# Differential attention in a two-block kernel: the softmax sum kept on VectorE, outputs copied unscaled in pairs, the norm taken once per head, and key copies moved to GpSimd

## The chip, the cores and the metric

The kernel runs on one core of a Trainium2 chip. The metric is the device time of one execution in microseconds. The engines are named as in the profile: PE is TensorE, PEld its weight loads, DVE is VectorE, ACT is ScalarE, POOL is GpSimd, SP is SyncE.

## The reference, cut to what matters

The program is a stack of transformer blocks on 512 tokens of width 1024, with 256 context tokens beside them. The change lies in one layer of the second part, whose mixer runs two attentions side by side: a neighbourhood attention with 8 heads of 64 columns, and a differential attention with 4 heads. A differential head has two queries and two keys of 64 columns and one value of 128 columns:

```python
def diff_attend(q1, q2, k1, k2, v, lam):
    scale = q1.shape[-1] ** -0.5
    p1 = jax.nn.softmax(jnp.einsum('bhqd,bhsd->bhqs', q1, k1).astype(F32) * scale, axis=-1)
    p2 = jax.nn.softmax(jnp.einsum('bhqd,bhsd->bhqs', q2, k2).astype(F32) * scale, axis=-1)
    return jnp.einsum('bhqs,bhsd->bhqd', (p1 - lam * p2).astype(v.dtype), v)
...
y_l = jnp.concatenate([merge_heads(ya_l), merge_heads(rms_norm(yb_l, subln) * (1.0 - lam_init))],
                      axis=-1) @ w_out
```

Tokens attend to 768 keys (512 tokens and 256 context), context tokens to the 256 context keys alone. Each output row of 128 columns is divided by its root mean square and multiplied by a gain row.

## The kernel before, in words

The layer's attentions are one software pipeline. `diff_attention` makes 24 items, 4 heads (`hd`) by 6 query tiles (`t`) of 128 rows: tiles 0 to 3 are **long** (768 keys, six blocks of 128), tiles 4 and 5 are **short** (256 keys, two blocks). `neighbourhood` adds its items behind them. `skewed` runs the list so that at step i the stage s of item i-s is issued, the deepest stage first; within that, the tile framework's scheduler decides the order in which each engine's queue takes the instructions. An engine takes its queue strictly in order.

The stages of a differential item, with the lines of the profile:

- `load`: at tile 0 of a head `stacked` prepares the head's keys (two f32r copies `whi`, `wlo`, whose other halves hold remainders, subtracted by GpSimd at L1585, and two high parts `kz`, copied by ScalarE at L1589, one per half of the partitions). For each tile `doubled` prepares the query: ScalarE copies, GpSimd subtracts `ql` (L1597) and twice `qd` (L1599). `stacked` with `kz` also serves the neighbourhood pairs and the dilated attention of the first block.
- `score`: for each of the two halves PE computes the scores (L1610) into one of two PSUM buffers, VectorE takes the row maximum (L900), ScalarE the exponential with its row sum (L901) into a tile `E`, VectorE the reciprocal of that sum (L904). Then VectorE makes the factor `er` (L1785) and adds the second exponential, times that factor, to the first: columns 0 to 511 on VectorE (L1787), columns 512 to 767 on GpSimd (a product L1791 and an addition L1792). Short items have the VectorE part only, of 256 columns.
- `turn`: PE transposes the sum (L436), ScalarE (L1628) and VectorE (L1630) copy the result from PSUM to the tile `PT`, of which there are three.
- `apply`: PE multiplies by the values into a `pv` bank (L1802), ScalarE copies the 128 columns to `da_o`, scaled by the reciprocal row sum (L1805), and squares them with a row sum (L1806).
- `norm`, once per head: VectorE works out the reciprocal root of 6 columns (L298 to L304, L1810) and multiplies the head's 128x768 tile `da_o` twice, by that root (L1812) and by the gain row (L1813).
- `end`, four steps later: PE transposes `da_o` (L436), and ScalarE and VectorE split it into the operand of the output projection (L319, L320).

After the last head the neighbourhood items follow in the same queues, so the last head's norm and end lie among them.

## Time and profile before

| what | us |
| --- | --- |
| runs | 2574.99, 2583.11, 2584.61 (median 2583.11) |
| profiled execution | 2572.39 |
| span of the profiled execution | 2570.6 |
| the differential items, in that span | about 1088 to 1206 |
| the last head's transposes of `da_o` | 1210.65 |

The profile is of one execution; all times in it are microseconds from the start of its span, or ns where marked. The rows of the page and of the trace on which the text rests stand in the section on rows. A busy column gives the time in which an engine was executing, with the number of instructions in brackets. PEclk is the granted share of full clock on TensorE. In a row of the order in time, the bracket at the end is how long the engine stood idle ahead of it, and whose result ended that.

### The profile page before, as it was taken

Reading aid. Unit: us, or ns where it says so; the run is one execution under the profiler, and the core shown is the slowest. Engines: PE = TensorE matmul, PEld = TensorE weight load, DVE = VectorE, ACT = ScalarE, POOL = GpSimd, SP = SyncE. Lnnn points to the kernel's source line nnn. Section 1 sums busy time; section 2 is a strip of 40 time slices with the busy share of each in tenths; the row PEclk is TensorE's granted clock in tenths of the full one; section 3 lists DMA queues with packets and bytes.
Section 4 is the critical chain, followed back from the end, with each engine's and each line's share of the span. In section 5 each row is a group of like instructions: output and inputs, shape, how many; then the busy total and the mean of one; then the engine's idle time right before and its main releaser. Section 6 shows DMA issues by size and latency. Waiting matters only on the chain.

```text
span 2570.6 us, 35341 instructions
## 1 busy us (share of the span) xinstructions
PE 2454.1 (95%) x13312; PEld 2036.7 (79%) x13312; DVE 1629.0 (63%) x2896; ACT 995.9 (39%) x1763; POOL 1197.7 (47%) x835
## 2 busy tenths in 40 slices
PE   8899999999999999877999999999999999999999
PEld 6668776878887777766888888888888888788887
DVE  6944648677775686588755876777576465534333
ACT  4435435322224423377633222122244563323222
POOL 3356536455556455587633332323245326344443
PEclk9999999999999899998999999999999999999999
DMA  5230023344444332301232333424242113232332
GB/s 192 74 111 14 29 72 131 117 166 138 152 162 138 132 107 85 103 17 32 72 120 82 121 138 107 140 92 155 74 132 82 34 60 138 82 95 84 106 101 91
DMA packets 105773, 262.13 MB, mean 102 GB/s; under 512 B 12017, under 2 KB 20337, under 8 KB 105220
## 3 DMA queue, kind: packets, MB, share of 16 engines
q1 hardware_dynamic: 105028, 258.84, 30.1%
q8 instruction: 105, 1.72, 0.3%
q10 hardware_dynamic: 576, 1.05, 0.1%
q14 instruction: 64, 0.52, 0.1%
HBM read 248.15 MB, written 16.93 MB: 103 GB/s over the span
## 4 chain that ended last, share of the span: by engine, by line
PE 75%; DVE 13%; POOL 3%; issue 3%; ACT 3%; DMA 2%; SPq 1%; POOLq 0%; ACTq 0%; DVEq 0%
PE ps_mm L326 15%; PE ps_mm L324 15%; PE ps_mm L325 15%; PE ps_mx L324 3%; PE ps_mx L325 3%; PE ps_mx L326 3%; PE ps_m L324 3%; PE ps_m L326 3%; PE ps_m L325 3%; PE ps_pv L1617 2%; PE ps_t L436 2%; PE ps_s L1610 2%; DVE cv_y L538 1%; POOL wlo L313 1%; PE ps_p L757 1%
## 5 line engine op out<-in xcount | busy, mean ns | idle before, releaser
L313 POOL TENSOR_TENSOR wlo<-wraw,whi 128x1024 fp32r<-128x1024 f32 (+2 forms) x344 | 783.5, 2281 | 1064.9 <-ACT whi L312 981.0
L312 ACT ACTIVATE whi<-wraw 128x1024 fp32r<-128x1024 f32 (+2 forms) x345 | 336.8, 978 | 892.0 <-PE ps_mm L325 470.1
L324 PE MATMUL ps_mm<-h,whi 128*128 128x512 f32 (+1 forms) x1496 | 539.9, 362 | 10.8 <-ACT whi L312 7.4
L326 PE MATMUL ps_mm<-h,wlo 128*128 128x512 f32 (+1 forms) x1496 | 538.6, 361 | 1.9 <-POOL wlo L313 1.9
L325 PE MATMUL ps_mm<-h,whi 128*128 128x512 f32 (+1 forms) x1496 | 538.9, 361 | 1.1 <-DVE h L1163 1.0
L324 PEld LDWEIGHTS ps_mm<-h,whi 128*128 128x128 f32 x1496 | 281.9, 189 | 56.5 <-ACT whi L312 7.4
L326 PEld LDWEIGHTS ps_mm<-h,wlo 128*128 128x128 f32 x1496 | 281.5, 188 | 49.2 <-POOL wlo L313 2.5
L325 PEld LDWEIGHTS ps_mm<-h,whi 128*128 128x128 f32 x1496 | 281.7, 188 | 46.4 <-DVE h L1163 1.5
L325 PE MATMUL ps_mm<-fa,whi 128*128 128x512 f32 (+1 forms) x528 | 187.5, 356 | 0.0
L326 PE MATMUL ps_mm<-fa,wlo 128*128 128x512 f32 (+1 forms) x528 | 186.2, 356 | 1.2 <-POOL wlo L313 1.2
L324 PE MATMUL ps_mm<-fa,whi 128*128 128x512 f32 (+1 forms) x528 | 185.6, 356 | 0.0
L1288 DVE SCALAR_TENSOR_TENSOR cb<-ps_mm,small,cb 128x511 f32<-128x511 f32 (+1 forms) x66 | 43.6, 660 | 186.8 <-ACT cb L1286 186.8
L1236 DVE SCALAR_TENSOR_TENSOR x<-ps_mm,mod,x 128x512 f32<-128x512 f32 x80 | 59.5, 749 | 136.6 <-PE ps_mm L326 129.7
L1109 DVE CUSTOM_DVE_ANT_0 ada_j<-ada_w,ada_c 128x512 f32<-128x512 f32 x128 | 134.5, 1051 | 7.0 <-DMA ada_w<-in_w_ada 6.7
L1109 DVE CUSTOM_DVE_ANT_0 ada_w<-ada_w,ada_c 128x512 f32<-128x512 f32 x128 | 129.5, 1012 | 3.5
L1109 DVE CUSTOM_DVE_ANT_0 x<-x 128x512 f32<-128x512 f32 x128 | 124.9, 996 | 1.9
L326 PEld LDWEIGHTS ps_mm<-fa,wlo 128*128 128x128 f32 x528 | 98.9, 188 | 17.8 <-POOL wlo L313 1.8
L324 PEld LDWEIGHTS ps_mm<-fa,whi 128*128 128x128 f32 x528 | 98.9, 188 | 16.4 <-ACT whi L312 0.3
L325 PEld LDWEIGHTS ps_mm<-fa,whi 128*128 128x128 f32 x528 | 99.2, 188 | 16.0
L900 DVE TENSOR_REDUCE nm<-ps_s 128x1 f32<-128x768 f32 (+1 forms) x96 | 73.9, 774 | 34.9 <-PE ps_s L1610 33.7
L436 PE MATMUL ps_t<-ident,E 128*128 128x128 f32 x464 | 77.7, 287 | 15.1 <-POOL E L1792 9.2
L325 PE MATMUL ps_mx<-h,whi 128*128 128x512 f32 x216 | 85.5, 396 | 3.8 <-DVE h L993 3.8
(500 smaller groups left out, 5207.5 us busy)
## 6 DMA issues: line engine op xcount, KB each, us to landing
wraw<-in_w_up SPq DMA_DIRECT2D x88, 512.0 KB
ada_w<-in_w_ada SPq DMA_DIRECT2D x128, 256.0 KB
wraw<-in_w_d SPq DMA_DIRECT2D x48, 384.0 KB
wraw<-in_w_d SPq DMA_DIRECT2D x53, 320.0 KB
x<-in_w_ada SPq DMA_DIRECT2D x64, 256.0 KB
wraw<-in_we_in SPq DMA_DIRECT2D x24, 512.0 KB
wraw<-in_w_g SPq DMA_DIRECT2D x22, 512.0 KB
wraw<-in_w_u SPq DMA_DIRECT2D x22, 512.0 KB
```

Source lines behind the costliest of these rows:

```text
L312: self.S.activation(hi[:, :n], raw[:, :n], AF.Copy)
L313: (eng or self.G).tensor_tensor(out=lo[:, :n], in0=raw[:, :n], in1=hi.bitcast(F32)[:, :n], op=ALU.subtract)
L324: mm(ps, lhi, rhi, start=start, stop=False)
L325: mm(ps, lhi, rlo, start=False, stop=False)
L326: mm(ps, llo, rhi, start=False, stop=stop)
L436: last = self.PE.transpose(ps[:, j * P:(j + 1) * P], src[:, j * P:(j + 1) * P], self.ident)
L900: V.tensor_reduce(out=m, in_=src, op=ALU.max, axis=AX.X, negate=True)
L1109: V.tensor_tensor_reduce(out=(junk, w)[s], in0=w, in1=c[:, s, i * T:i * T + T], scale=0.5, scalar=0.0, op0=ALU.mult, op1=ALU.add, accum_ou ...
L1236: V.scalar_tensor_tensor(out=xs[s][:, m], in0=p[:, :w], scalar=mod[:, gate * 8 + m, s:s + 1], in1=xs[s][:, m], op0=ALU.mult, op1=ALU.add)
L1288: V.scalar_tensor_tensor(out=cb[:, t0 + 1:t1], in0=pg[s][:, :w_ - 1], scalar=fw[0], in1=cb[:, t0 + 1:t1], op0=ALU.mult, op1=ALU.add)
L1610: self.PE.matmul(p[:, c0:min(n, c0 + 512)], q[i], k[i][:, c], start=i == 0, stop=i == 1)
L1617: self.PE.matmul(pv[64 * e:64 * e + 64, cols], vals(e, kt), pts[e][:, kt * P:(kt + 1) * P], start=kt == 0, stop=kt == nk - 1)
```

## The change

The sum of the two exponentials is made by one VectorE instruction over all columns, 768 or 256; the two GpSimd instructions are gone. The reciprocal row sums of the first half are kept for a whole head in a tile `da_r`. The `pv` bank is one PSUM bank for the whole stage with four slots of 128 columns, and ScalarE copies two items' outputs at once, unscaled (128x256); it squares nothing. The norm is then taken per head: GpSimd squares the 128x768 tile (L1810 of the kernel after), VectorE sums it by tiles (L1812), multiplies twice by `da_r` (L1814), works out the root and multiplies it by `da_r` (L1817), and GpSimd does the two products over 128x768 (L1818, L1819). `end` comes two steps later than before. In `stacked` the two `kz` copies are made by GpSimd instead of ScalarE; this holds for all callers (24 copies in the program).

```diff
         for e, (own, other) in enumerate(HALVES):
-            self.S.activation(kz[own, e], src[own], AF.Copy)
+            self.G.tensor_copy(kz[own, e], src[own])
...
-                    c = slice(0, min(n, T))
-                    V.scalar_tensor_tensor(out=e1[:, c], in0=e2[:, c], scalar=r2, in1=e1[:, c], op0=ALU.mult,
+                    V.scalar_tensor_tensor(out=e1[:, :n], in0=e2[:, :n], scalar=r2, in1=e1[:, :n], op0=ALU.mult,
                                            op1=ALU.add)
-                    if n > T:
-                        c = slice(T, n)
-                        G.tensor_scalar(out=e2[:, c], in0=e2[:, c], scalar1=r2, scalar2=None, op0=ALU.mult)
-                        G.tensor_tensor(out=e1[:, c], in0=e1[:, c], in1=e2[:, c], op=ALU.add)
...
-                    pv = self.bank(ps, "pv")
+                    if hd == t == 0:
+                        st["v"] = self.bank(ps, "pv")
...
+                    c = (6 * hd + t) % 4 * P
                     for kt in range(nk):
-                        PE.matmul(pv[:, :P], st["t", hd, t][:, kt * P:(kt + 1) * P],
+                        PE.matmul(st["v"][:, c:c + P], st["t", hd, t][:, kt * P:(kt + 1) * P],
                                   vb[:, kt + k0 // P, hd * P:(hd + 1) * P], start=kt == 0, stop=kt == nk - 1)
-                    sq = at.tile([P, P], F32, name="da_q", bufs=1)
-                    S.activation(st["o", hd][:, t], pv[:, :P], AF.Copy, scale=r1)
-                    S.activation(sq, st["o", hd][:, t], AF.Square, accum_out=st["s", hd][:, t:t + 1])
+                    if t % 2:
+                        S.activation(st["o", hd][:, t - 1:t + 1].rearrange("p a b -> p (a b)"), st["v"][:, c - P:c + P],
+                                     AF.Copy)
...
+                    sq = at.tile([P, 6 * P], F32, name="PT", bufs=3)
+                    G.tensor_tensor(out=sq, in0=flat, in1=flat, op=ALU.mult)
+                    ssq = at.tile([P, 6], F32, name="da_s")
+                    V.tensor_reduce(out=ssq, in_=sq.rearrange("p (a b) -> p a b", b=P), op=ALU.add, axis=AX.X)
+                    for _ in range(2):
+                        V.tensor_tensor(out=ssq, in0=ssq, in1=r1, op=ALU.mult)
                     V.tensor_scalar(out=ssq, in0=ssq, scalar1=1.0 / P, scalar2=EPS, op0=ALU.mult, op1=ALU.add)
                     r = self.rsqrt(at, ssq, 6, "da")
-                    V.tensor_tensor(out=o, in0=o, in1=self.lastb(r, P), op=ALU.mult)
-                    V.tensor_tensor(out=o, in0=o, in1=self.midb(sub, 6), op=ALU.mult)
+                    V.tensor_tensor(out=r, in0=r, in1=r1, op=ALU.mult)
+                    G.tensor_tensor(out=o, in0=o, in1=self.lastb(r, P), op=ALU.mult)
+                    G.tensor_tensor(out=o, in0=o, in1=self.midb(sub, 6), op=ALU.mult)
...
                 items.append([load, None, score, None, turn, apply, norm if last else None, None, None, None,
...
-                              end if last else None])
+                              None, None, end if last else None])
```

The order that results is shown at two places. The first is GpSimd's queue where the scores pass from head 1 to head 2. `kz1` and `kz0` are the two sets of high parts, `qkb1` holds the queries and keys of heads 2 and 3, `kaT` the keys of the neighbourhood pairs; the number behind a name is the tile. Before:

```order
L1597 TENSOR_TENSOR ql_9260<-qkb1_7081,qd_9259 128x128 [waits PE_49,Activation_49]
L1599 TENSOR_TENSOR qd_9259<-qkb1_7081,ql_9260 64x128 [waits Pool_49]
L1599 TENSOR_TENSOR qd_9259<-qkb1_7081,ql_9260 64x128
L1791 TENSOR_SCALAR E_9191<-E_9191,er_9196 128x256 [waits DVE_49,Activation_49,Pool_49]
L1597 TENSOR_TENSOR ql_9309<-qkb1_7081,qd_9308 128x128 [waits PE_49,Activation_49]
L1585 TENSOR_TENSOR whi_9921<-kaT_7067,whi_9921 64x768 [waits Activation_49,Pool_49]
L1792 TENSOR_TENSOR E_9179<-E_9179,E_9191 128x256 [waits Pool_49]
L1599 TENSOR_TENSOR qd_9308<-qkb1_7081,ql_9309 64x128 [waits Pool_49]
L1599 TENSOR_TENSOR qd_9308<-qkb1_7081,ql_9309 64x128
L1585 TENSOR_TENSOR wlo_9922<-kaT_7067,wlo_9922 64x768 [waits Activation_49]
```

The first three rows prepare tile 0 of head 2 (`qd_9259`), and between them and tile 1 (`qd_9308`) stand the two halves of the last long item's sum. After:

```order
L1597 TENSOR_TENSOR ql_9213<-qkb1_7081,qd_9212 128x128 [waits PE_49,Activation_49,Pool_49]
L1589 CAST kz1_8689<-qkb1_7081 64x768 [waits PE_49]
L1599 TENSOR_TENSOR qd_9212<-qkb1_7081,ql_9213 64x128 [waits Pool_49]
L1599 TENSOR_TENSOR qd_9212<-qkb1_7081,ql_9213 64x128
L1585 TENSOR_TENSOR whi_9818<-kaT_7067,whi_9818 64x768 [waits Activation_49]
L1597 TENSOR_TENSOR ql_9257<-qkb1_7081,qd_9256 128x128 [waits PE_49,Pool_49]
L1589 CAST kz1_8689<-qkb1_7081 64x768 [waits Pool_49]
L1585 TENSOR_TENSOR wlo_9819<-kaT_7067,wlo_9819 64x768 [waits Activation_49]
L1597 TENSOR_TENSOR ql_9301<-qkb1_7081,qd_9300 128x128 [waits PE_49,Pool_49]
L1599 TENSOR_TENSOR qd_9256<-qkb1_7081,ql_9257 64x128 [waits Pool_49]
L1599 TENSOR_TENSOR qd_9256<-qkb1_7081,ql_9257 64x128
```

The sum is gone from the queue, and a copy into `kz1`, which waits for PE's last scores of head 1, now stands ahead of the query of tile 0 (`qd_9212`); a second copy and both key subtractions stand ahead of that of tile 1 (`qd_9256`). From head 2 to head 3 the queue after has the same shape, with the product L1819 between the first copy and tile 0's two L1599.

The second place is the end of the last head, among the first neighbourhood items. On GpSimd after:

```order
L1589 CAST kz0_8688<-kaT_7067 64x768 [waits PE_49]
L1597 TENSOR_TENSOR ql_10299<-qaT_7066,qd_10298 128x128 [waits PE_49,Activation_49,Pool_49]
L1589 CAST kz0_8688<-kaT_7067 64x768 [waits Pool_49]
L1585 TENSOR_TENSOR whi_10892<-kaT_7067,whi_10892 64x768 [waits Activation_49]
L1818 TENSOR_TENSOR da_o_9730<-da_o_9730,rsq_i_10013 128x768 [waits DVE_49,Pool_49]
L1585 TENSOR_TENSOR wlo_10893<-kaT_7067,wlo_10893 64x768 [waits Activation_49,Pool_49]
L1599 TENSOR_TENSOR qd_10298<-qaT_7066,ql_10299 64x128 x2
L1819 TENSOR_TENSOR da_o_9730<-da_o_9730,brow_67 128x768 [waits Pool_49]
```

On PE at that place after, where `kz0` is the set that the copies above overwrite:

```order
L1610 MATMUL ps_s_10270<-wlo_9819,qd_10188 128x256 [waits Activation_49,Pool_49]
L1610 MATMUL ps_s_10270<-kz0_8688,ql_10189 128x256
L1617 MATMUL ps_pv_10028<-PT_10141,vw1_9843 64x128 [waits DMAHW5_49,DMAHW4_49,DMAHW6_49,DMAHW3_49,DVE_49]
L1610 MATMUL ps_s_10287<-whi_10244,qd_10252 128x256 [waits Activation_49,Pool_49]
L1610 MATMUL ps_s_10287<-kz1_8689,ql_10253 128x256
L1610 MATMUL ps_s_10287<-whi_10244,qd_10252 128x256
L1610 MATMUL ps_s_10287<-kz1_8689,ql_10253 128x256
L436 MATMUL ps_t_10159<-ident_68,da_o_9730 128x128 [waits PE_49,Pool_49]
```

The last reader of `kz0` (second row) stands five matmuls ahead of the transposes of `da_o`, and these now wait for GpSimd's L1819, at the end of the queue above. Before, the same transposes waited for VectorE's L1813:

```order
L1610 MATMUL ps_s_10346<-whi_9921,qd_10299 128x256 [waits Activation_49,Pool_49]
L1610 MATMUL ps_s_10346<-kz0_8688,ql_10300 128x256
L436 MATMUL ps_t_10220<-ident_68,da_o_9676 128x128 [waits DVE_49]
L436 MATMUL ps_t_10220<-ident_68,da_o_9676 128x128 x3
L436 MATMUL ps_t_10227<-ident_68,da_o_9676 128x128 x2
```

What moved is the engine whose queue the transposes wait for, and what stands in that queue ahead of their operand.

## Rows read from the trace of the kernel before

**Rows 1.** The page: its first line and section 1.

```profile
span 2570.6 us, 35341 instructions
...
PE 2454.1 (95%) x13312; PEld 2036.7 (79%) x13312; DVE 1629.0 (63%) x2896; ACT 995.9 (39%) x1763; POOL 1197.7 (47%) x835
```

**Rows 2.** Windows: length, busy PE, PEld, DVE, ACT, POOL (instructions); PEclk, DMA share, GB/s.

```profile
1109.00:1192.60 83.60, 64.06 (x403) 55.84 (x404) 71.44 (x170) 68.14 (x188) 66.64 (x89) 0.92 0.09 26
1122.00:1128.00 6.00, 4.80 (x37) 4.19 (x37) 6.00 (x17) 4.69 (x12) 5.08 (x9) 1.00 0.02 4
1218.00:1282.00 64.00, 62.78 (x612) 51.62 (x609) 47.33 (x137) 46.47 (x125) 41.14 (x66) 1.00 0.18 56
```

**Rows 3.** Costliest groups of VectorE by shape, 1086 to 1212.

```profile
L900 DVE TENSOR_REDUCE nm<-ps_s 128x1 f32<-128x768 f32 x32 | 30.4, 951 | 24.0 <-PE ps_s L1610 23.6
L1787 DVE SCALAR_TENSOR_TENSOR E<-E,er 128x512 f32<-128x512 f32 x16 | 12.6, 790 | 0.2
L1785 DVE SCALAR_TENSOR_TENSOR er<-er,lam,es 128x1 f32<-128x1 f32 x24 | 10.7, 445 | 0.3
...
L1787 DVE SCALAR_TENSOR_TENSOR E<-E,er 128x256 f32<-128x256 f32 x8 | 7.1, 892 | 0.4
...
L1812 DVE TENSOR_TENSOR da_o<-da_o,rsq_i 128x768 f32<-128x768 f32 x4 | 4.3, 1082 | 0.1
...
L301 DVE TENSOR_TENSOR rsq_a<-rsq_i,rsq_a 128x6 f32<-128x6 f32 x12 | 3.2, 266 | 0.0
```

**Rows 4.** Groups of GpSimd by shape, 1086 to 1206.

```profile
L1599 POOL TENSOR_TENSOR qd<-qkb,ql 64x128 fp32r<-64x128 f32 x44 | 23.1, 525 | 3.2
L1791 POOL TENSOR_SCALAR E<-E,er 128x256 f32<-128x256 f32 x16 | 18.8, 1176 | 5.5 <-DVE er L1785 2.3 <-ACT da_o L1805 1.0 <-ACT E L901 0.7
...
L1792 POOL TENSOR_TENSOR E<-E 128x256 f32<-128x256 f32 x16 | 11.6, 726 | 0.7
...
L1585 POOL TENSOR_TENSOR whi<-qkb,whi 64x768 fp32r<-64x768 f32 x2 | 3.7, 1828 | 0.2
```

**Rows 5.** Groups of GpSimd by shape, whole span.

```profile
L586 POOL TENSOR_TENSOR sgate<-gth,brow 128x512 f32<-128x512 f32 x4 | 5.6, 1402 | 4.7 <-DVE rsq_i L559 4.0 <-DVE gth L584 0.6
...
L709 POOL TENSOR_TENSOR kd<-gdn,kdf 128x512 f32<-128x512 f32 x4 | 4.1, 1042 | 5.5 <-PE ps_c L811 5.4
L1561 POOL TENSOR_TENSOR kl<-gkT,kh 128x768 fp32r<-128x768 f32 x2 | 3.7, 1852 | 0.1
...
L1852 POOL COPY kdup<-qk_raw 128x768 f32<-128x768 f32 x2 | 1.6, 830 | 0.7 <-DVE qk_raw L1419 0.7
```

**Rows 6.** Busy time of the instructions on `da_o`, 1086 to 1212 (PE, PEld, VectorE, ScalarE).

```profile
1086.00:1212.00 126.00, 5.16 (x24) 4.04 (x24) 10.13 (x8) 18.28 (x72) 0.93 0.08 24
```

**Rows 7.** PE in order of time at the two passages from head to head.

```profile
1131.83 0.41 PE L1610 MATMUL ps_s<-wlo,qd 128*128 128x256 f32 x1
...
1136.69 0.44 PE L436 MATMUL ps_t<-ident,E 128*128 128x128 f32 x2 [2.66 <-POOL E L1792]
1139.61 0.77 PE L1610 MATMUL ps_s<-whi,qd 128*128 128x512 f32 x1
...
1143.70 0.47 PE L1610 MATMUL ps_s<-whi,qd 128*128 128x512 f32 x1 [0.67 <-POOL qd L1599]
...
1159.20 0.36 PE L1610 MATMUL ps_s<-wlo,qd 128*128 128x256 f32 x1
...
1164.30 0.62 PE L1610 MATMUL ps_s<-whi,qd 128*128 128x512 f32 x1
...
1168.94 0.40 PE L1610 MATMUL ps_s<-whi,qd 128*128 128x512 f32 x1
```

**Rows 8.** PE, VectorE and GpSimd in order of time, the last head's end.

```profile
1210.65 1.54 PE L436 MATMUL ps_t<-ident,da_o 128*128 128x128 f32 x6 [4.99 <-DVE da_o L1813]
...
1208.16 2.44 DVE L1813 TENSOR_TENSOR da_o<-da_o,brow 128x768 f32<-128x768 f32 x1
...
1207.38 2.40 POOL L1585 TENSOR_TENSOR whi<-kaT,whi 64x768 fp32r<-64x768 f32 x1
```

More of the change, by code (lines that the diff above doesn't have):

```diff
@@ L1775, in score @@
                     if t == 0:
-                        st["o", hd] = at.tile([P, 6, P], F32, name="da_o")
-                        st["s", hd] = at.tile([P, 6], F32, name="da_s")
+                        st["r", hd] = at.tile([P, 6], F32, name="da_r")
                     es = []
@@ L1782, in score @@
                         self.scores(p, (q[:, e], lo), (k[e][:, k0:], kz[e][:, k0:]))
-                        es.append(self.exp_rows(at, p[:, :n], n, None, TC, bufs=4))
-                    (e1, r1, s1), (e2, r2, _) = es
+                        es.append(self.exp_rows(at, p[:, :n], n, None, TC, None if e else st["r", hd][:, t:t + 1], 4))
+                    (e1, _, s1), (e2, r2, _) = es
                     V.scalar_tensor_tensor(out=r2, in0=r2, scalar=lam, in1=s1, op0=ALU.mult, op1=ALU.mult)
-                    c = slice(0, min(n, T))
@@ L1793, in score @@
-                    st["e", hd, t] = e1, r1
+                    st["e", hd, t] = e1
                 def turn(hd=hd, t=t, nk=nk):
-                    st["t", hd, t] = self.pt_tiles(at, ps, st["e", hd, t][0], nk)
+                    st["t", hd, t] = self.pt_tiles(at, ps, st["e", hd, t], nk)
                 def apply(hd=hd, t=t, k0=k0, nk=nk):
-                    pv = self.bank(ps, "pv")
-                    r1 = st["e", hd, t][1]
+                    if hd == t == 0:
+                        st["v"] = self.bank(ps, "pv")
@@ L1801, in apply @@
+                    if t == 0:
+                        st["o", hd] = at.tile([P, 6, P], F32, name="da_o")
+                    c = (6 * hd + t) % 4 * P
                     for kt in range(nk):
-                        PE.matmul(pv[:, :P], st["t", hd, t][:, kt * P:(kt + 1) * P],
+                        PE.matmul(st["v"][:, c:c + P], st["t", hd, t][:, kt * P:(kt + 1) * P],
                                   vb[:, kt + k0 // P, hd * P:(hd + 1) * P], start=kt == 0, stop=kt == nk - 1)
-                    sq = at.tile([P, P], F32, name="da_q", bufs=1)
@@ L1805, in apply @@
-                    S.activation(st["o", hd][:, t], pv[:, :P], AF.Copy, scale=r1)
-                    S.activation(sq, st["o", hd][:, t], AF.Square, accum_out=st["s", hd][:, t:t + 1])
+                    if t % 2:
+                        S.activation(st["o", hd][:, t - 1:t + 1].rearrange("p a b -> p (a b)"), st["v"][:, c - P:c + P],
+                                     AF.Copy)
                 def norm(hd=hd):
-                    ssq, o = st["s", hd], st["o", hd]
+                    o, r1 = st["o", hd], st["r", hd]
@@ new lines, in norm @@
+                    flat = o.rearrange("p a b -> p (a b)")
+                    sq = at.tile([P, 6 * P], F32, name="PT", bufs=3)
[4 more added lines that the diff above has]
+                        V.tensor_tensor(out=ssq, in0=ssq, in1=r1, op=ALU.mult)
```

## The prediction

> **What bounds the kernel now.** I read the page first: TensorE is busy for 95% of the span [rows 1], so the time is TensorE's work plus the places where it waits. The differential items are such a place. In the window of three heads, 83.6 us, VectorE is the busiest engine with 71.4, ahead of ScalarE 68.1, GpSimd 66.6 and TensorE 64.1; in six microseconds in the middle of a run of long items VectorE shows 6.00 of 6.00 [rows 2]. The reader is to see a stage bound by VectorE while long items run, with 83.6 - 71.4 = 12.2 us of VectorE idleness elsewhere. The order in time shows where: at a passage from head to head. After the last score of head 1 at 1131.83 the first score of head 2 comes at 1139.61 and that of its tile 1 at 1143.70; between head 2 and head 3 the same rows are 1159.20, 1164.30 and 1168.94 [rows 7]. At the first of the two TensorE stands still for 2.66 us for GpSimd's part of the sum, in the second row of that group. Behind the stage the neighbourhood items run at 62.78 of 64 us of TensorE [rows 2], except for one hole of 4.99 us, in which TensorE waits for the last head's `da_o` [rows 8].
>
> So four things are to be priced: VectorE's work per head, what holds VectorE up, the passages, and the hole at the end.
>
> **VectorE's work.** Added: 16 long sums grow from 512 columns at 0.790 to 768. No row has that form; the nearest is the product of two 768-column operands L1812 at 1.082, so 16 x 0.292 = +4.7 (by the ratio of columns it would be 1.185 and +6.3, an upper bound) [rows 3]. Four reductions over 768 columns, priced by the row maximum at 0.951: +3.8. Three small products per head, 12 at L301's 0.266: +3.2 [rows 3]. Removed: the eight products L1812 and L1813, 10.1 [rows 6]. Net +1.6, between 0 (small operations in gaps) and +3.2. All of it counts, since VectorE is full there.
>
> **ScalarE's work.** It loses most of the 18.3 us on `da_o` [rows 6] and eight `kz` copies, and gains twelve pair copies. I cost this at nothing: VectorE is the fuller engine. Were ScalarE the cover that sets the exponentials' pace, it would be a gain; that is in the first rival.
>
> **GpSimd's work.** Removed: 18.8 + 11.6 = 30.4 us [rows 4]. Added per head: the square, by a 128x768 two-operand row, 1.85; the product with a column broadcast, L709's 1.042 for 512 columns times 1.5, 1.56; the product with a row broadcast, L586's 1.402 times 1.5, 2.10 [rows 5]. Four heads: 22.0. Eight copies into `kz` in the stage at 0.83, a plain GpSimd copy's row [rows 5]; the subtraction of the same shape L1585 takes 1.83 [rows 4], the other bound. 8 x 0.83 = 6.6. Together 28.6, or 1.8 less than before. The other 16 copies lie in stages where TensorE is full (62.78 of 64 in the neighbourhood window [rows 2]); there they cost nothing so long as the queues behind them, the queries' `qd`, are ready ahead of TensorE. Without that cover each would cost up to 0.83.
>
> **What holds VectorE up.** Some VectorE rows are longer than their shape: L1785, one column, takes 0.445 beside L301's 0.266 for six; the 256-column sum takes 0.892 where half of the 512-column one, with some start cost, would be 0.47 [rows 3]; the last L1813 took 2.44 us, while GpSimd's L1585 ran for 2.40 from 0.8 us earlier [rows 8], against L1812's 1.082 for the same size. All read two operands from SBUF, and run beside GpSimd. The excess is 24 x 0.18 + 8 x 0.42 = 7.7 us, and for the four L1813, whose sum is 10.1 - 4.3 = 5.8 against 4.3, another 1.5 [rows 3, 6]: 9.2. A VectorE instruction that meets a GpSimd one waits for what is left of it, on average half its length, so the cost goes with the sum of the squares of GpSimd's durations. Per head these are 4 x (1.18 squared + 0.73 squared) = 7.7 that go, 1.85, 1.56 and 2.10 squared and two times 0.83 squared = 11.6 that come, beside about 13 for queries and keys (11 L1599 at 0.525, half as many of the like L1597, and two and a half L1585 at 1.83) [rows 4, 5]: 20.7 becomes 24.6, a factor of 1.19. So 9.2 x 0.19 = +1.8; bounds 0 and the second rival's.
>
> The Trainium skill has a rule on this (SBUF — State Buffer, Who interferes with whom): a VectorE instruction with two SBUF inputs contends with a GpSimd instruction that reads SBUF, one of them blocks fully, and a reduction never does on this chip. The trace agrees where it shows L1813 at 2.44 beside 2.40 of GpSimd [rows 8]; L1812's unstretched mean says that not every meeting costs [rows 3]. By the rule taken for every meeting the time would be the second rival's, by the rows' mean it is +1.8.
>
> **The passages.** They are walked along GpSimd's queue as the order shows it, from the release by the last scores (0.4 us). Head 1 to 2: a copy 0.83 and two `qd` 1.05, so tile 0 is ready at 2.3 instead of 7.8; then a subtraction 1.83, `ql` at about the price of a `qd`, 0.53, a copy 0.83, 1.83, 0.53 and 1.05, so tile 1 at 8.9 instead of 11.9. Head 2 to 3: the 2.10 of L1819 stand ahead too, tile 0 at 4.4 instead of 5.1, tile 1 at 11.0 instead of 9.7 [rows 4, 5, 7]. By tile 0 that is -6.2 in all, by tile 1 -1.7. VectorE can use an early tile 0 only until it runs dry waiting for tile 1, so the worth lies between, and nearer to tile 1's: I take -3. With copies at 1.83, tile 1 is later by 2.0 at either passage: +2.3, the other bound. Head 0 to 1 I take as unchanged: two halves of a sum go from that queue and two copies come.
>
> **The hole.** The transposes of the last `da_o` wait behind this queue, from the last reader of `kz0`: 0.83 + 0.53 + 0.83 + 1.83 + 1.56 + 1.83 + 1.05 + 2.10 = 10.6 us [rows 4, 5]. TensorE has five matmuls of at most 0.41 to do meanwhile [rows 7], about 1 us as they overlap. It stands for 9.6 instead of 4.99: +4.6; bounds 0, if GpSimd's products run ahead of the copies, and +7 with copies at 1.83. Queued behind them on TensorE are the neighbourhood's transposes and scores, so nothing hides it.
>
> **Sum.** 1.6 + 1.8 - 3 + 4.6 = +5.0 us. On the profiled execution, 2572.4 (1.8 us around its span of 2570.6 [rows 1]), that is 2577.4. That execution is faster than the three runs; the mean of all four is 2578.8, so I put the expected time at 2584, close to the runs' median of 2583.1. Half a per cent, 12.9 us, is about what a measurement here tells from no change.
>
> **The rivals.**
>
> *GpSimd's part of the sum is what paces the stage (faster).* For it: TensorE's 2.66 us wait for it, and tile 0 of head 2 late by 7.8 us [rows 7]. Then VectorE's 12.2 us of idleness go, half of its 9.2 us of excess too since no GpSimd work lies inside an item's own chain, and the hole is hidden: 1.6 - 12.2 - 4.6 = -15.2, so 2564. Against it: the key subtractions and query work that fill GpSimd at the passages stay, and two copies join them. Chance 0.25.
>
> *GpSimd blocks VectorE (slower).* Its place is the long items: the full-width sum reads two SBUF operands, and each of the five new GpSimd instructions per head meets one. L1813 was held for 2.44 - 1.08 = 1.36 of a 2.40 us instruction, 57% [rows 8]; half of 4 x 7.2 us is 14.4 in place of 1.8, and the sum is +17.6, so 2596. It decides from 9.7 us upwards, where the sum passes 12.9. Against it: GpSimd's total falls by 1.8 and before, 30.4 us of sum parts went with only 9.2 of excess. Chance 0.17.
>
> *No measurable change*, with the terms as above or each a few microseconds off: 0.58; its own range, from the terms' bounds without their extremes together, is 2573 to 2596.
>
> So: faster 0.25, same 0.58, slower 0.17. Range 2563 to 2600: the lower end takes in the first rival, the upper the second with the copies' bound on top.
>
> **What the changed profile would show.** VectorE stays full in the middle of the long items, with the sum near 1.1 us. The waits of TensorE's transposes for GpSimd's L1792 are gone, and the waits at the passages name GpSimd's `qd` and `ql`, with tile 1's first scores about 9 and 11 us behind the last ones. The `kz` copies take 0.8 us (1.8 would be the other bound), L1819 about 2.1. TensorE waits some 10 us ahead of the last `da_o`, released by GpSimd. The prediction is wrong if that hole stays at 5 us, if VectorE's idleness falls by much more than 3 us, or if the sum takes 1.4 us or more.

## The result, and the profile after

The changed kernel is slower: 2608.72 us (median of 4 runs, 2607.51 to 2610.2) against 2582.31 us for the four runs of before, which spread over 9.6 us. The ratio on record is 1.0125 with a 95% interval of 1.0105 to 1.0146. It is not that of the two medians, which are 26 us apart: 1.25% is 32 us, and about as much, 31 to 33 us, lies between the changed kernel and the 15 to 23 runs of before that were taken beside each group of experiments (medians 2575.84 to 2577.89). The text goes by the 32 us. The forecast was no change, 2584, in a range that ended at 2600. The profiled execution has a span of 2605.7 us, 35.1 longer than that of before [rows 1]. The page's busy times:

```profile
PE 2462.7 (95%) x13312; PEld 2040.0 (78%) x13312; DVE 1634.5 (63%) x2904; ACT 968.6 (37%) x1679; POOL 1206.5 (46%) x839
```

The busy times answer almost exactly to those of before: TensorE +8.6 us, VectorE +5.5, ScalarE -27, GpSimd +9. No engine has 32 us more work; the time went into waiting. Where it went is read from one mark per head, the first score of tile 1, which both kernels have. First the two marks of before that the rows ahead do not hold (the others are 1143.70 and 1168.94 [rows 7]), and between them the last score of head 0, in TensorE's order of time:

```profile
1091.47 0.50 PE L1610 MATMUL ps_s<-whi,qd 128*128 128x512 f32 x1 [1.27 <-ACT E L901]
...
1108.03 0.38 PE L1610 MATMUL ps_s<-wlo,qd 128*128 128x256 f32 x1 [0.15 <-ACT E L901]
...
1114.91 0.48 PE L1610 MATMUL ps_s<-whi,qd 128*128 128x512 f32 x1
```

And the four of after, with the last scores of heads 0 and 1 between them (that of head 2 is in the excerpts below):

```profile
1091.11 0.48 PE L1610 MATMUL ps_s<-whi,qd 128*128 128x512 f32 x1 [1.38 <-issue]
...
1105.93 0.28 PE L1610 MATMUL ps_s<-wlo,qd 128*128 128x256 f32 x1
...
1118.70 0.78 PE L1610 MATMUL ps_s<-whi,qd 128*128 128x512 f32 x1
...
1138.52 0.36 PE L1610 MATMUL ps_s<-wlo,qd 128*128 128x256 f32 x1
...
1151.30 0.78 PE L1610 MATMUL ps_s<-whi,qd 128*128 128x512 f32 x1
...
1187.92 0.77 PE L1610 MATMUL ps_s<-whi,qd 128*128 128x512 f32 x1
```

The stage starts at the same time. A step from head to head took 23.4, 28.8 and 25.2 us before, 77.5 in all, and takes 27.6, 32.6 and 36.6 now, 96.8 in all: 19.3 us are lost over three steps. Most of it lies at the passages. From the last score of a head to the first of the next head's tile 1 it took 6.9, 11.9 and 9.7 us before and takes 12.8, 12.8 and 18.1 now, 15.1 more in all; the other 4.2 lie inside the heads. Behind the steps comes the hole ahead of the last `da_o`, in TensorE's order of time:

```profile
1241.33 0.90 PE L436 MATMUL ps_t<-ident,da_o 128*128 128x128 f32 x3 [9.61 <-POOL da_o L1819]
```

It is 9.61 us instead of 4.99 [rows 8], 4.6 more. What follows the neighbourhood items in both kernels is the output projection. Its first matmul, before and after:

```profile
1280.33 0.50 PE L324 MATMUL ps_mm<-h,whi 128*128 128x512 f32 x1
```

```profile
1308.02 0.50 PE L324 MATMUL ps_mm<-h,whi 128*128 128x512 f32 x1
```

From tile 1 of the last head to there 120.1 us pass instead of 111.4 (1280.33 less 1168.94 [rows 7]), 8.7 more with the hole among them. The remaining 7.4 us of the 35.1 lie behind it, outside the stage; the runs of one kernel differ by as much.

The passage from head 2 to head 3 shows how it is lost. Three excerpts in order of time, TensorE, VectorE and GpSimd of the changed kernel:

```profile
1169.84 0.36 PE L1610 MATMUL ps_s<-wlo,qd 128*128 128x256 f32 x1
...
1175.19 0.41 PE L436 MATMUL ps_t<-ident,E 128*128 128x128 f32 x2 [1.41 <-DVE E L1785]
...
1176.01 0.72 PE L1610 MATMUL ps_s<-whi,qd 128*128 128x512 f32 x1
...
1184.36 1.51 PE L436 MATMUL ps_t<-ident,E 128*128 128x128 f32 x6 [4.69 <-DVE E L1785]
...
1172.41 1.83 DVE L1784 SCALAR_TENSOR_TENSOR er<-er,lam,es 128x1 f32<-128x1 f32 x1
...
1172.43 1.80 POOL L1585 TENSOR_TENSOR whi<-kaT,whi 64x768 fp32r<-64x768 f32 x1
...
1179.82 0.45 POOL L1597 TENSOR_TENSOR ql<-qkb,qd 128x128 fp32r<-128x128 f32 x1 [2.19 <-PE ps_s L1610]
1180.35 0.98 POOL L1599 TENSOR_TENSOR qd<-qkb,ql 64x128 fp32r<-64x128 f32 x2
```

Two things are to be seen. First, tile 0's score comes at 1176.01, only behind the transposes of the old head's last sum at 1175.19, and tile 1's at 1187.92 behind the transposes of tile 0's own sum at 1184.36, for which TensorE waits 4.69 us; tile 1's query has been ready since 1181.33, when the `qd` of the last row ends. Twice the pipeline of items runs empty. Tile 0's transposes stand ahead of tile 1's scores at all three passages (TensorE waits 1.17 and 3.21 us for them at the first two). Second, VectorE's factor, an operation on one column, takes 1.83 us beside a GpSimd subtraction of 1.80.

The first is a matter of TensorE's queue, which the text ahead of the result did not print. There, with the numbers of tiles, before (first rows of groups only: L1610 of head 3, L436 on the sums of heads 2 and 3):

```order
L1610 MATMUL ps_s_9678<-whi_9586,qd_9594 128x512 [waits Activation_49]
...
L436 MATMUL ps_t_9672<-ident_68,E_9567 128x128 [waits Activation_49]
...
L1610 MATMUL ps_s_9690<-wlo_9587,qd_9594 128x512 [waits Activation_49]
...
L1610 MATMUL ps_s_9723<-whi_9586,qd_9643 128x512 [waits PE_49,Activation_49,Pool_49]
...
L436 MATMUL ps_t_9719<-ident_68,E_9624 128x128 [waits DVE_49,PE_49]
...
L436 MATMUL ps_t_9764<-ident_68,E_9683 128x128 [waits DVE_49]
```

and after:

```order
L436 MATMUL ps_t_9577<-ident_68,E_9493 128x128 [waits DVE_49,PE_49]
...
L436 MATMUL ps_t_9616<-ident_68,E_9545 128x128 [waits DVE_49,PE_49]
...
L1610 MATMUL ps_s_9582<-whi_9511,qd_9519 128x512 [waits Pool_49]
...
L436 MATMUL ps_t_9667<-ident_68,E_9587 128x128 [waits DVE_49,PE_49]
...
L1610 MATMUL ps_s_9620<-whi_9511,qd_9563 128x512 [waits PE_49,Pool_49]
```

Before, tile 0's scores (`qd_9594`) stand ahead of or among the last two old transposes, and tile 1's scores (`qd_9643`) ahead of the transposes of tile 0's sum (`E_9683`). After, both old sums are transposed first, then tile 0 is scored, then its sum (`E_9587`) is transposed, and only then is tile 1 (`qd_9563`) scored.

### The profile page after: what moved, and what is told of

Read it like the earlier page. It is cut to its first block, busy times and chain, and to the rows that moved or that the text cites. A ratio compares the mean times of both kernels' runs of the same rounds, so it can differ in the third digit from the quotient of the medians.

```text
span 2605.7 us, 35268 instructions
## 1 busy us (share of the span) xinstructions
PE 2462.7 (95%) x13312; PEld 2040.0 (78%) x13312; DVE 1634.5 (63%) x2904; ACT 968.6 (37%) x1679; POOL 1206.5 (46%) x839
## 4 chain that ended last, share of the span: by engine, by line
PE 74%; DVE 14%; ACT 3%; issue 3%; POOL 3%; DMA 2%; SPq 0%; ACTq 0%; POOLq 0%; DVEq 0%
PE ps_mm L324 15%; PE ps_mm L326 15%; PE ps_mm L325 15%; PE ps_mx L324 3%; PE ps_mx L325 3%; PE ps_mx L326 3%; PE ps_m L326 3%; PE ps_m L324 3%; PE ps_m L325 3%; PE ps_pv L1617 2%; PE ps_t L436 2%; PE ps_s L1610 2%; DVE h L1163 1%; DVE E L1785 1%; DVE cv_y L538 1%
## 5 line engine op out<-in xcount | busy, mean ns | idle before, releaser
L1288 DVE SCALAR_TENSOR_TENSOR cb<-ps_mm,small,cb 128x511 f32<-128x511 f32 (+1 forms) x66 | 43.6, 660 | 190.0 <-ACT cb L1286 190.0
L436 PE MATMUL ps_t<-ident,E 128*128 128x128 f32 x464 | 76.0, 290 | 22.1 <-DVE E L1785 16.7
```

The lines of the kernel that those rows point to most:

```text
L436: last = self.PE.transpose(ps[:, j * P:(j + 1) * P], src[:, j * P:(j + 1) * P], self.ident)
L1288: V.scalar_tensor_tensor(out=cb[:, t0 + 1:t1], in0=pg[s][:, :w_ - 1], scalar=fw[0], in1=cb[:, t0 + 1:t1], op0=ALU.mult, op1=ALU.add)
```

## The experiments

The theories, as the runs went: **A**, the changed order on TensorE lets the items' pipeline run empty. **B** (e1 to e4), what costs is GpSimd's own time, by its late queue and by holding VectorE. From e5 on B is split: **C**, GpSimd's queue stands ahead of the queries; **D**, GpSimd's reads hold VectorE. Ratios are to the kernel before, run on the same chip, with 95% intervals. "Steps" is the sum of the three head steps of the profiled execution (77.5 before, 96.8 after). "Held" is the whole busy time of VectorE's factor and sums, the rows that GpSimd may hold, 128x1, 128x256 and 128x768 or 128x512 (30.4 before: 12.6 + 10.7 + 7.1 [rows 3]).

| run | median us | ratio | interval | steps | held |
| --- | --- | --- | --- | --- | --- |
| changed kernel | 2608.72 | 1.0125 | 1.0105 to 1.0146 | 96.8 | 41.7 |
| e1 kz on ScalarE | 2585.7 | 1.0039 | 1.0022 to 1.0055 | 77.2 | 36.0 |
| e2 order forced by the exponential | 2604.29 | 1.0107 | 1.0085 to 1.013 | 89.7 | 42.4 |
| e3 e1 with a drain | 2592.8 | 1.0059 | 1.004 to 1.0077 | 83.2 | 35.4 |
| e4 kz alone on GpSimd | 2587.59 | 1.0045 | 1.0032 to 1.0058 | 82.9 | 30.3 |
| e5 e1 with copies again | 2599.46 | 1.0094 | 1.0068 to 1.012 | 86.0 | 40.6 |
| e6 e1 with zeros | 2589.44 | 1.0047 | 1.0031 to 1.0063 | 81.5 | 36.5 |
| e7 e1, products on VectorE | 2579.31 | 1.0011 | 1.0 to 1.0021 | 76.0 | 28.1 |
| e8 sum alone | 2574.99 | 0.9986 | 0.9969 to 1.0004 | 74.8 | 28.8 |
| e9 order put right by the query | 2597.56 | 1.0079 | 1.0063 to 1.0096 | 84.4 | 40.4 |
| e10 nothing of it on GpSimd | 2575.29 | 1.0001 | 0.9988 to 1.0015 | 74.9 | 29.0 |
| e11 norm alone | 2585.42 | 1.0031 | 1.0016 to 1.0046 | 77.6 | 34.0 |
| e12 e1 with the early end | 2583.96 | 1.0033 | 1.0017 to 1.0049 | 77.1 | 36.8 |
| e13 e9 with zeros | 2587.55 | 1.0037 | 1.0023 to 1.0051 | 74.2 | 34.9 |

**e1, the copies back on ScalarE.**

```diff
-            self.G.tensor_copy(kz[own, e], src[own])
+            self.S.activation(kz[own, e], src[own], AF.Copy)
```

> The changed kernel with the kz copies back on ScalarE, all else as changed. Theory A (order): GpSimd's two copies at each passage made the scheduler put the transposes of a new head's tile 0 ahead of tile 1's scores in TensorE's queue, so the item pipeline runs empty once per head; the trace after shows tile 1's query ready 5.0, 6.0 and 6.5 us before its scores start. With the copies gone the order is tile 1's scores first again: those 17.5 us, some 2 us of queue and 1.7 us of the last hole go, so about 2588 us (2608.7 before this edit). Theory B (GpSimd's own time, by its queue being late and by blocking VectorE): only the copies' own 0.83 us each go, two per passage and two at the hole, so about 2602.

2585.7 us: 22 us of the 32 come with the `kz` copies. There are 24 of them in the program; the ten between the first passage and the hole take 0.82 to 1.57 us each. TensorE's marks of e1:

```profile
1084.70 0.50 PE L1610 MATMUL ps_s<-whi,qd 128*128 128x512 f32 x1 [1.27 <-ACT E L901]
...
1109.81 0.47 PE L1610 MATMUL ps_s<-whi,qd 128*128 128x512 f32 x1 [0.81 <-ACT E L901]
...
1137.30 0.48 PE L1610 MATMUL ps_s<-whi,qd 128*128 128x512 f32 x1
...
1161.88 0.77 PE L1610 MATMUL ps_s<-whi,qd 128*128 128x512 f32 x1
```

The steps are 25.1, 27.5 and 24.6: the passages cost what they cost before, and at each of them tile 1's scores are back ahead of the transposes of tile 0's sum (at the first, 1109.81 and 1111.23 against 1113.70). This is far from B's 2602 and near A's 2588; but the copies' removal takes away GpSimd's work and its reads too, so the next two try the order by itself.

**e2, the order forced, and e3, a drain put into e1.** In e2 the transposes of tile 0 of heads 1 to 3 get an extra matmul, into the bank that they overwrite, that reads the first exponential of tile 1. In e3 tile 1's first score gets one that reads the sum of tile 0.

```diff
+            if after is not None and k0 == 0:
+                self.PE.matmul(p[:, :P], after[:, :P], after[:, :P], start=True, stop=True)
...
+                        if hd and t == 1 and e == 0:
+                            d = st["e", hd, 0][:, :P]
+                            PE.matmul(p[:, :P], d, d, start=True, stop=True)
```

> The changed kernel with kz still on GpSimd, but for heads 1 to 3 a small extra matmul (overwritten afterwards) makes the transposes of tile 0 wait for the first exponential of tile 1, which puts tile 1's scores ahead of them on TensorE. GpSimd's work is unchanged. Theory A: most of the 17.5 us go, less what tile 0's transposes now come later, so 2592 to 2599. Theory B: nothing is gained, 2608 or slower.

> The kernel of e1 (kz on ScalarE) with, for heads 1 to 3, an extra matmul (overwritten afterwards) that makes tile 1's first score wait for the sum of tile 0: the empty pipeline is put back without any work on GpSimd. Theory A: 15 to 18 us slower than e1, so about 2605. Theory B: within 4 us of e1.

e2 gained about 5 us and e3 cost 5 to 7 against e1; both intervals overlap with those of the kernels that they are held against, so neither is clear. Both miss A's numbers. They are less telling than they were meant to be: e2 makes tile 0's transposes later than tile 1's exponential, which gives back elsewhere what it saves (its three passages take 29.8 us instead of 43.6, the stretches inside the heads 59.8 instead of 53.2), and e3 rebuilds only the second of the two dry places, without GpSimd beside it. So A was left in doubt, and its size open.

**e4, the copies alone on the kernel before.**

```diff
-            self.S.activation(kz[own, e], src[own], AF.Copy)
+            self.G.tensor_copy(kz[own, e], src[own])
```

> The kernel before with the kz copies on GpSimd alone. Theory A: the order shows tile 0's transposes ahead of tile 1's scores at all three passages here too, so about 15 us slower than before, 2597. Theory B: eight copies of 0.83 us, of which those at the passages count, so 3 to 6 us slower, about 2587.

2587.59 us, 11 us slower than before: between A's 15 and B's 3 to 6. The same edit costs half of what it costs together with the rest of the change.

**e5, the copies as mere cost, and e6, zeros in their place.** In both ScalarE makes the copies; GpSimd writes the same values once more (e5), or zeros into the half that holds zeros (e6).

```diff
             self.S.activation(kz[own, e], src[own], AF.Copy)
+            if n > T:
+                self.G.tensor_copy(kz[own, e], src[own])
...
             self.S.activation(kz[own, e], src[own], AF.Copy)
+            if n > T:
+                self.G.memset(kz.bitcast(F32)[other, e], 0.0)
```

> The kernel of e1 (kz on ScalarE) with GpSimd writing the same values into kz once more, for the differential and neighbourhood keys: GpSimd's copies are back as a cost, ScalarE's stay. Theory C: what costs is that GpSimd's queue stands ahead of the next head's queries, and so is on the path at each passage. Then most of the 22 us between the changed kernel and e1 come back: 2600 or more. Theory A alone (order on TensorE, by e2 and e3 worth 5 to 7 us): the order has the drain at one or two passages of three, +2 to +5, about 2590.

> As e5, but what GpSimd writes instead is zeros into the other half of kz, which holds zeros already: the same place in the queue, the same waits, 0.74 us each instead of 0.83, and no read from SBUF. Theory C: within 3 us of e5. Theory D: what costs is that VectorE's sums and factors, which read two operands from SBUF, are held while a GpSimd instruction reads (the 256-column sum took 2.1 us at a passage beside a 1.8 us GpSimd subtraction). Then e6 is 5 us or more faster than e5, about 2590.

e5 came near C's 2600, e6 10 us below it, as D had it. But their orders differ too: in e5 both old sums are transposed ahead of tile 0's scores at the passage from head 2 to 3, in e6 not. And of the difference only 4.5 us lie in the steps; 6.7 lie between tile 1 of the last head and the last `da_o` (56.1 us in e5, 49.4 in e6). What the pair does show is in the held rows, 40.6 with copies and 36.5 with zeros. So e5 and e6 do not separate A from D; e13 was made for that.

**e7, the norm's products back on VectorE, and e8, the sum alone.** e7 is e1 with the two products on VectorE, e8 the kernel before with the one-instruction sum.

```diff
-                    G.tensor_tensor(out=o, in0=o, in1=self.lastb(r, P), op=ALU.mult)
-                    G.tensor_tensor(out=o, in0=o, in1=self.midb(sub, 6), op=ALU.mult)
+                    V.tensor_tensor(out=o, in0=o, in1=self.lastb(r, P), op=ALU.mult)
+                    V.tensor_tensor(out=o, in0=o, in1=self.midb(sub, 6), op=ALU.mult)
```

> The kernel of e1 with the two 128x768 products of the norm on VectorE as before; the square stays on GpSimd. VectorE gains 8 products, 8 to 10 us, GpSimd loses 13. Theory C and D: GpSimd's queue at the passages is shorter by one product of 2 us or more each, and fewer reads hold VectorE: 3 to 8 us faster than e1, 2578 to 2582. If VectorE's work alone sets the pace (the forecast's reckoning): 8 us slower than e1, 2594.

> The kernel before with the whole sum on VectorE and nothing else changed. VectorE gains 16 x 0.27 us, GpSimd loses 30 us that stood ahead of the queries and held VectorE. Theory C and D: 3 to 12 us faster than before. By VectorE's work alone: 4 us slower than before.

e7 was 6 to 7 us faster than e1, though VectorE got 10.5 us of products more. e8 was 4 us faster than before by the medians, though VectorE got 4.6 us more; its interval just reaches no change. Both speak against a reckoning by VectorE's work. VectorE's groups by shape in e7:

```profile
L1785 DVE SCALAR_TENSOR_TENSOR E<-E,er 128x768 f32<-128x768 f32 x16 | 16.6, 1037 | 0.1
L1784 DVE SCALAR_TENSOR_TENSOR er<-er,lam,es 128x1 f32<-128x1 f32 x24 | 6.8, 284 | 0.3
...
L1785 DVE SCALAR_TENSOR_TENSOR E<-E,er 128x256 f32<-128x256 f32 x8 | 4.7, 592 | 0.1
```

and in the changed kernel:

```profile
L1785 DVE SCALAR_TENSOR_TENSOR E<-E,er 128x768 f32<-128x768 f32 x16 | 19.6, 1226 | 0.2
L1784 DVE SCALAR_TENSOR_TENSOR er<-er,lam,es 128x1 f32<-128x1 f32 x24 | 14.7, 613 | 0.5
...
L1785 DVE SCALAR_TENSOR_TENSOR E<-E,er 128x256 f32<-128x256 f32 x8 | 7.4, 924 | 0.2
```

The same 48 instructions take 28.1 us in the one and 41.7 in the other.

**e9, the order put right by the query.** The changed kernel whole; an extra matmul, overwritten at once, lets the transposes of a head's last two tiles wait for the next head's first query, and those of its tile 0 for the query of tile 1. A query is ready just when its scores can start, so unlike e2 nothing is made late.

```diff
-                    st["t", hd, t] = self.pt_tiles(at, ps, st["e", hd, t], nk)
+                    nx = (hd, 1) if hd and t == 0 else (hd + 1, 0) if hd < 3 and t >= 4 and True else None
+                    st["t", hd, t] = self.pt_tiles(at, ps, st["e", hd, t], nk, nx and st[("q", *nx)][0][:, 0])
...
+            if after is not None and k0 == 0:
+                self.PE.matmul(p[:, :P], after, after, start=True, stop=True)
```

> The changed kernel, kz on GpSimd, nothing taken from any engine. An extra matmul (overwritten afterwards) makes the transposes of tiles 4 and 5 of a head wait for the query of the next head's tile 0, and those of tile 0 for the query of its tile 1. That alone puts the next scores ahead of them on TensorE at the three passages, without waiting for any exponential as e2 did. Theory A, in the form that e2, e3 and e5 leave (the changed order has two places at a passage where the pipeline runs dry: old transposes ahead of tile 0's scores, tile 0's transposes ahead of tile 1's): the passages, 12.8, 16.8 and 18.1 us in the changed kernel, shrink to what GpSimd's queue takes, about 8, 9 and 11, so 15 to 20 us faster, 2589 to 2594. Theory D (GpSimd's reads hold VectorE, whatever the order): the held time stays, 2602 or more.

2597.56 us, a ratio of 1.0079: 0.46% or 12 us faster than the changed kernel, short of A's 15 to 20. Its marks:

```profile
1096.14 0.77 PE L1610 MATMUL ps_s<-whi,qd 128*128 128x512 f32 x1 [1.38 <-issue]
...
1121.55 0.48 PE L1610 MATMUL ps_s<-whi,qd 128*128 128x512 f32 x1
...
1151.04 0.50 PE L1610 MATMUL ps_s<-whi,qd 128*128 128x512 f32 x1 [0.97 <-POOL qd L1599]
...
1180.50 0.78 PE L1610 MATMUL ps_s<-whi,qd 128*128 128x512 f32 x1
```

The steps fall from 96.8 to 84.4, 12.4 us, as much as the time does, while VectorE's held rows stay at 40.4 (41.7). The order is thus shown as a cause by itself, of some 12 us, and that is not its whole size: e9 puts only the first half of tile 1's scores ahead of tile 0's transposes. At the passage from head 0 to 1 these still stand ahead of the second half (1125.88), and TensorE waits for them:

```profile
1124.68 1.54 PE L436 MATMUL ps_t<-ident,E 128*128 128x128 f32 x6 [2.13 <-DVE E L1787]
```

GpSimd's queue was sorted anew as well. At the passage from head 2 to 3 both products of the norm now stand behind the last scores and ahead of tile 1's query, so this does not help e9. The 16.8 us in the expectation run from the first half of head 1's last item; from its last score, as for the other two, the passage took 12.8. The third mark now waits for GpSimd's `qd`, which is what the walk along its queue had assumed of all of them.

**e13, e9 with zeros.** GpSimd writes zeros instead of copying, so the high parts of these keys are left out. The order on TensorE is not quite that of e9: at the passages from head 0 to 1 and from 1 to 2 tile 0's transposes move behind both halves of tile 1's scores.

```diff
+            if n > T:
+                self.G.memset(kz.bitcast(F32)[own, e], 0.0)
+            else:
+                self.G.tensor_copy(kz[own, e], src[own])
```

> The kernel of e9 (order put right, kz on GpSimd) with GpSimd writing zeros in place of the copies for the differential and neighbourhood keys: the keys' high parts are left out, the place and the waits in GpSimd's queue stay, 0.74 us instead of 0.83 each and no read from SBUF. Theory D (reads hold VectorE): VectorE's factors and sums, 40 us in e9, fall towards the 36 of e1, and the time by 5 to 8 us, about 2591. Theory C (the place in the queue): 1 to 2 us faster than e9.

2587.55 us, 1.0037: 10 us faster than e9, beyond D's 5 to 8 and far from C's 1 to 2. VectorE's groups by shape in e9 and in e13:

```profile
L1787 DVE SCALAR_TENSOR_TENSOR E<-E,er 128x768 f32<-128x768 f32 x16 | 18.3, 1142 | 0.2
L1786 DVE SCALAR_TENSOR_TENSOR er<-er,lam,es 128x1 f32<-128x1 f32 x24 | 13.7, 572 | 0.4
L1787 DVE SCALAR_TENSOR_TENSOR E<-E,er 128x256 f32<-128x256 f32 x8 | 8.4, 1056 | 0.2
```

```profile
L1790 DVE SCALAR_TENSOR_TENSOR E<-E,er 128x768 f32<-128x768 f32 x16 | 17.1, 1066 | 0.2
L1789 DVE SCALAR_TENSOR_TENSOR er<-er,lam,es 128x1 f32<-128x1 f32 x24 | 9.0, 376 | 0.4
L1790 DVE SCALAR_TENSOR_TENSOR E<-E,er 128x256 f32<-128x256 f32 x8 | 8.8, 1099 | 0.1
```

The held rows fall by 5.5 us, 4.7 of them in the factor on one column. The marks of e13, and tile 0's transposes at the first passage:

```profile
1097.86 0.50 PE L1613 MATMUL ps_s<-whi,qd 128*128 128x512 f32 x1 [1.33 <-ACT E L901]
...
1119.74 0.50 PE L1613 MATMUL ps_s<-whi,qd 128*128 128x512 f32 x1 [0.80 <-ACT E L901]
...
1123.90 0.87 PE L436 MATMUL ps_t<-ident,E 128*128 128x128 f32 x6
...
1142.99 0.48 PE L1613 MATMUL ps_s<-whi,qd 128*128 128x512 f32 x1
...
1172.02 0.79 PE L1613 MATMUL ps_s<-whi,qd 128*128 128x512 f32 x1
```

The steps are 21.9, 23.3 and 29.0, together 74.2 instead of 84.4. In e9 they were 25.4, 29.5 and 29.5. So the gain lies at the two passages where TensorE's order changed with the edit, and at the third, where it hardly did, the step falls by 0.4 us only. GpSimd's queue is sorted differently too: at the first passage tile 1's query stands ahead of a key subtraction of 1.8 us that was ahead of it in e9. A zero moreover takes about 0.1 us less than a copy and needs no source. How much of the 10 us is held time is therefore not shown. What is shown is the 5.5 us in the rows. The Trainium skill (SBUF — State Buffer, Who interferes with whom) has it that a VectorE instruction with two SBUF inputs contends with a GpSimd instruction that reads SBUF and not with one that only writes it; e13 against e9 agrees, with 5.5 us in the rows.

**e10, e11 and e12.** e10 is e7 with the square on ScalarE and `end` at its old step, e11 the changed kernel with sum and copies as before (the norm, the pair copies and the later end alone), e12 is e1 with `end` at its old step.

```diff
-                    G.tensor_tensor(out=sq, in0=flat, in1=flat, op=ALU.mult)
+                    S.activation(sq, flat, AF.Square)
...
-                              None, None, end if last else None])
+                              end if last else None])
```

> What the runs so far favour: the whole sum on VectorE, pairs copied unscaled, norm per head with the square on ScalarE and the products on VectorE, kz on ScalarE, end back at its old step; GpSimd has no part in sum, norm or kz. Theories A and D: no drained passage, fewest reads of GpSimd, so no slower than e8 (0.9986 of before) and up to 8 us faster than before. By VectorE's work alone (+8 us over e1): 2585 or more.

> The changed kernel with the sum split as before and kz on ScalarE: the norm per head on GpSimd, the pair copies and the later end alone. If the three parts add up (all three 32 us, kz alone 11.6, sum alone -3.6): 24 us slower than before. If kz's cost is an interaction with the rest (22 us on top of sum and norm, e1 10 us above before): e1's 10 us plus the sum's 3.6, so about 14 us slower than before, 2592.

> The kernel of e1 with `end` four steps behind the norm as before, instead of six. In e1 the heads' steps are back at those of before, and the remaining 10 us lie between head 3's tile 1 and the end of the neighbourhood items. If the later transposes of da_o cost them (they stand among items that leave TensorE no gap): 4 to 8 us faster than e1, about 2579. If GpSimd's products cost them, by being late behind its queue: the transposes wait longer, same as e1 or up to 5 us slower.

e10 is at 1.0001: no version found beats the kernel before beyond its interval, and e8 comes nearest. e11 costs 8 to 10 us, less than either of its expectations; with kz alone (11) and the sum alone (-4) the parts add up to some 16 of the 32, so half of the loss is interaction. e12 gains nothing clear over e1 (1.0033 against 1.0039): the later end is not what e1's 10 us are. Taking GpSimd out of the products (e7) recovers 7 of them. They lie behind the heads: from tile 1 of the last head to the output projection e1 takes 122.0 us and e7 116.3, against 111.4 before.

## Why the prediction was wrong, step by step

**The passages, -3 us, is the step that failed.** It walked along GpSimd's queue from the last scores to the next queries and took for granted that TensorE would start a score once its query was there. Measured were +15.1 us at the three passages; the one from head 0 to 1, taken as unchanged, is 5.9 of them. GpSimd's costs were about as walked: the copies took 0.86 to 0.97 us on average (0.83 in the text), the squares 1.59, the products 1.47 and 2.01 (1.85, 1.56 and 2.10). The queries of tile 1 were there 6.8 and 11.5 us behind the last score at the later two passages (8.9 and 11.0 in the text). That the second comes so near is luck in part: 2.19 us of it are a wait of GpSimd's queue for tile 0's own late scores (1179.82), which the walk did not have. But TensorE started the scores of tile 1 only 5.0, 6.0 and 6.6 us after their queries were there. What failed is that the copies also made the scheduler, which orders every engine's queue, put transposes ahead of scores on TensorE. The printed order showed it; the text looked it up on GpSimd and at the last hole, not on TensorE at the passages. e9 prices the part that it puts right at 12 us.

**What holds VectorE up, +1.8 us, was mis-sized.** That GpSimd's instructions lengthen VectorE's is borne out. In the changed kernel factor and sums take 41.7 us; about the shortest that the runs show for them is 16.6 (e7) + 6.8 (e7) + 4.0 (e8's short sums, 506 ns by eight) = 27.4, so 14.3 are held. Before it was 30.4 less 12.6 + 6.8 + 4.0, or 7.0. In busy time the term is +7.3: 4.0 of it in the factor, 3.0 in the long sums, 0.3 in the short ones. Pricing it by the squares of GpSimd's durations over the whole stage did not see where the meetings fall: the factor of 1.83 us stands at a passage. A passage is one chain from a score over exponential, factor and sum to the transposes, so held time there should delay the next link; how much of the time it is was not separated from the order (e5 and e6, e9 and e13). The base of 9.2 also held 1.5 us of the products L1812 and L1813, which the change takes off VectorE; without them the text's own reckoning gives 1.5. The rival that named this as the way to slower gave 2596. Its mechanism is real, but it put it in the full-width sums of the long items, and most of it is in the factor.

**VectorE's own work, +1.6 us**, was about right in its prices: the reduction 0.943 (0.951), the sum 1.04 in e7 (1.082), though 1.23 in the changed kernel. That it all counts was wrong: e7 and e8 add VectorE work and lose no time.

**ScalarE's relief at nothing** is not contradicted: it has 27 us less to do, and the time still rose. No run tests it alone.

**The hole, +4.6 us, came out as worked out in length**: 9.61 instead of 4.99, released by GpSimd's L1819, with the queue in the printed order. That it is worth 4.6 us of time is not shown. In e1 the hole is 4.96 us again, and yet from tile 1 of the last head to the output projection e1 takes 122.0 us against 120.1 in the changed kernel.

**The rival on the faster side** rested on GpSimd's part of the sum pacing the stage. e8 takes that part away alone: its steps fall by 2.7 us and its time by 3.6, with an interval from 8 us faster to 1 us slower. So it is worth about half of the rival's 15 us at most, and possibly nothing.

**The signs of being wrong** that the prediction named were a hole that stays at 5 us, VectorE's idleness falling by much more than 3 us, and a sum of 1.4 us or more. None of them came: the hole is 9.61 us, the sum takes 1.23, and VectorE's idleness in the window of three heads rose from 12.2 to 22.3 us. What missed were the 9 and 11 us that it gave for tile 1's scores behind the last ones: they came after 12.8 and 18.1, and the waits there name VectorE's sum, not GpSimd's queries.

**The sum of it.** From 1.0125 the order takes 0.46% (e9) and what e13 changes 0.42%, together as much as moving the copies off GpSimd (e1, 0.86%). The 0.42% stay open between the rest of TensorE's order, GpSimd's queue and its reads. Of the remaining 0.4%, GpSimd's two products are 0.28% (e1 to e7). What then remains, 0.11% with an interval from 0, is not told apart from nothing. How the products cost it was not taken apart further. The hole ahead of the last `da_o` is not it (4.96 us in e1, 5.43 in e7); VectorE's held rows fall from 36.0 to 28.1.

## What to carry to other kernels

A small instruction moved to another engine's queue is priced by what a scheduler then does with every queue: print the order of the engine that consumes, at the place where the pipeline is thinnest, and look for a consumer of late results that now stands ahead of a producer of the next ones. Where work is moved to GpSimd, look at VectorE's two-operand instructions that lie on a chain beside it, and not only at the mean over the stage: here the factor's mean rose from 0.445 to 0.613 us, but at one passage it took 1.83. And when an order is put right by an edit, read the queues again before the next edit is measured against it: e13 differed from e9 in more than what GpSimd read.

## What the runs showed of the hardware

A VectorE instruction on one column took 1.83 us beside a GpSimd subtraction of 1.80, against 0.284 on the average where GpSimd read little (e7). VectorE's held rows fell from 40.6 to 36.5 us where GpSimd wrote zeros in place of copies (e5, e6), and from 40.4 to 34.9 (e9, e13). TensorE's granted clock fell where it ran dry. Windows of the changed kernel: length, busy TensorE, its weight loads, VectorE, ScalarE, GpSimd with instructions in brackets, granted clock, DMA share and GB/s.

```profile
1109.00:1209.60 100.60, 69.34 (x399) 59.48 (x398) 78.31 (x173) 53.76 (x131) 61.65 (x76) 0.85 0.08 22
1231.70:1241.30 9.60, 0.02 (x1) 0.00 (x0) 0.00 (x0) 0.00 (x0) 9.08 (x9) 0.63 0.00 0
1241.30:1248.00 6.70, 6.54 (x38) 5.25 (x40) 2.45 (x7) 3.65 (x9) 0.48 (x1) 0.52 0.08 22
```

Over the three passages the grant is 0.85, against 0.92 before [rows 2]; in the 6.7 us behind the hole, where TensorE had stood still for 9.6 us, it is 0.52, near the lower of the two levels, 1.2 of 2.4 GHz. The first 512-column scores of tile 1 took 0.77 to 0.78 us at the three passages, against 0.40 to 0.48 before (where tile 0's took 0.77 and 0.62 at the later two [rows 7]). So a place where TensorE runs dry is paid for a second time when it starts again. Some 5 us of the loss may be this, an estimate: about 400 matmuls around the passages keep TensorE busy for 69.34 us instead of 64.06 [rows 2].
